# Pairs of channel tiles by Strassen's products, and down sums in DRAM, in layer 0's FFN of a two-layer backbone

## The chip, the cores and the metric

The kernel runs on one core of one Trainium2 chip. The metric is the device time of one execution in microseconds. The engines are named as in the profile: PE (TensorE), DVE (VectorE), ACT (ScalarE), POOL (GpSimd) and SP (SyncE, which only issues DMAs here).

## What is computed

Two layers of a trunk over 256 latent and 256 context tokens, 2048 wide, float32. Layer 0 has a pooling mixer, layer 1 neighbourhood attention; each is followed by a gated FFN (5504 wide) with a depthwise convolution over three neighbouring tokens on its gate. In layer 0 both streams go through the FFN:

```python
def conv_ffn(u, w_gate, w_up, conv_w, conv_b, w_down):
    T = u.shape[1]
    gp = jnp.pad(u @ w_gate, ((0, 0), (1, 1), (0, 0)))
    gte = gp[:, :T] * conv_w[0] + gp[:, 1:T + 1] * conv_w[1] + gp[:, 2:] * conv_w[2] + conv_b
    return (jax.nn.silu(gte) * (u @ w_up)) @ w_down
...
    for i in range(DEPTH):
        ml = (silu_c @ w_mod[i] + b_mod[i]).reshape(B, 6, 1, D)
        mc = (silu_cc @ w_mod[i] + b_mod[i]).reshape(6, 1, 1, D)
...
        h = h + ml[:, 5] * conv_ffn(modulate(rms_norm(h, norm2_g[i]), ml[:, 3], ml[:, 4]),
                                    ffn_w_gate[i], ffn_w_up[i], ffn_conv_w[i], ffn_conv_b[i], ffn_w_down[i])
        if not last:
...
            hc = hc + mc[5] * conv_ffn(modulate(rms_norm(hc, norm2_g[i]), mc[3], mc[4]),
                                       ffn_w_gate[i], ffn_w_up[i], ffn_conv_w[i], ffn_conv_b[i], ffn_w_down[i])
```

## The kernel before

All products are done in a short float format, fp32r, with each operand split into a high part and the rest (hi and lo). A product is three matmuls: hi with hi, hi with lo, lo with hi. A weight tile comes by a DMA of 512 KB (128x1024, `load`, L127), ACT casts it to the high part (L143), and DVE subtracts that from it for the low part (L145). The tokens lie as 16 tiles A0 to A15 of 128 features by 512 columns (256 latent, 256 context), hi and lo, made by `normalise` (L304 to L317).

The FFN of layer 0 has 43 channel tiles f of 128. `gu0(f)` does gate and up of one tile, each 16 input tiles × 3 matmuls of 128x512 (L631 to L633) into one PSUM bank. `gate0` (L362 to L380) makes the convolution and the product on ACT and DVE: a scaled copy (L364), two additions of the shifted bank (L366, L368), Silu (L371), times up (L372), split in hi and lo (L378, L379). Gate and up of tiles 0 to 7 are done earlier, in another form; the change touches tiles from 11 on.

`down0(c, ...)` takes a chunk of four channel tiles: for each of 16 output tiles, 4 × 3 matmuls of 128x512 (L657 to L659). ACT scales each half of the result (latent, context) by the modulation (L669), and POOL adds it to the residual streams hl and hc, which lie in SBUF (L670). The last chunk adds on DVE instead (L663) and starts the next norm. The main loop (L674 to L702) does gate and up of chunk c, then down of chunk c − 1.

Beside this runs a pump, `mod_pairs`: modulation rows of layer 1, made on DVE. One step loads 512 KB of `wmod` and multiplies and adds it into `macc`, by four operations of 512 columns or one of 1024 (L239, L241); at a row's end come transposes (L251) and reduces (L252). The generator is advanced at written places in `gu0` and `down0`.

Buffers around the change: six places for loaded weights, of which the pump has three in this stage; four pairs of hi and lo tiles (128x1024); seven tiles for the FFN's activations; PSUM with four banks for gate and up and four for down. Each engine works through its own queue in order. A scheduler sets that order when the program is built; a tile that is reused makes its next writer wait.

Of the kernel before, what the change touches and what calls it, by code (L numbers as in the profile page):

```python
# [10 lines left out]
F32 = mybir.dt.float32  # L11
F32R = mybir.dt.float32r
AF = mybir.ActivationFunctionType
ALU = mybir.AluOpType
# [3 lines left out]
P = 128  # L18
D = 2048
KT = D // P  # L20
T = 256
F = 5504
NF = F // P
H = 32
W = 64
# [5 lines left out]
NS = 8  # L31
# [26 lines left out]
def kernel(ctx: ExitStack, tc: tile.TileContext, xT, cxT, wmod, wg, wu, wd, wp,  # L58
                         wq, wv, wo, vec, cc, rope, inv, strips, out):
    nc = tc.nc  # L60
    main = ctx.enter_context(tc.tile_pool(name="main", bufs=1))
    wst = ctx.enter_context(tc.tile_pool(name="wst", bufs=1))
    whp = ctx.enter_context(tc.tile_pool(name="whp", bufs=3))
# [34 lines left out]
    hl = main.tile([P, KT, T], F32, name="hl")  # L98


    extra = []
    turn = [0]

    hold = []

# [15 lines left out]
    def load(src, cols, name):  # L121

        ts = []
        for j in range(0, cols, 1024):
            n = min(1024, cols - j)
            t = stage(f"{name}_{j}")
            nc.sync.dma_start(t[:, :n], src(j, j + n))  # L127
            ts.append((t, n))
        return ts

    def split(ts, name, share=0):

        parts = []
        for j, (t, n) in enumerate(ts):
            turn[0] += 1
            pools = [whp] * 3 + extra
            pool = pools[turn[0] % len(pools)]
            hi = pool.tile([P, 1024], F32R, tag="wh", name=f"{name}h{j}")
            lo = pool.tile([P, 1024], F32R, tag="wl", name=f"{name}l{j}")
            with ExitStack() as behind:  # L140
                for ins in hold:
                    behind.enter_context(tc.issue_after(ins))
                nc.scalar.copy(hi[:, :n], t[:, :n])  # L143
                eng = nc.gpsimd if share and turn[0] % share == 0 else nc.vector
                eng.tensor_tensor(lo[:, :n], t[:, :n], hi[:, :n].bitcast(F32), op=ALU.subtract)  # L145
            parts.append((hi, lo))
        return parts
# [7 lines left out]
    both = (0, 1)  # L155
# [146 lines left out]
    A = {}  # L302
# [15 lines left out]

    chunks = [list(range(f, min(f + 4, NF))) for f in range(0, NF, 4)]


    v_first = []
    with ExitStack() as ph0:
        p0 = ph0.enter_context(tc.tile_pool(name="p0", bufs=1, reuse_waits="tile"))
        f0 = ph0.enter_context(tc.tile_pool(name="f0", bufs=6, reuse_waits="tile"))
        hc = p0.tile([P, KT, T], F32, name="hc")
# [7 lines left out]
        def h_of(s):  # L334
            return hc if s else hl
# [2 lines left out]
            return f0.tile([P, 2, 512], dt, tag="act", bufs=7, name=name)  # L338

        PART = {}  # L340
        sc = p0.tile([P, KT, 32], F32, name="sc")
# [278 lines left out]
        def gu0(f):  # L620
            res = []
            for nm, wsrc in (("g", wg), ("u", wu)):
                parts = ld(wsrc[0, f], f"w{nm}0_{f}")
                if f > NS + 3:
                    next(pump, None)
                ps = bank("gu", f"{nm}0_{f}")
                for k in range(KT):
                    hi, lo = parts[k // 8]
                    c = P * (k % 8)
                    xh, xl = flat(A[k][:, 0]), flat(A[k][:, 1])  # L630
                    nc.tensor.matmul(ps, hi[:, c : c + P], xh, start=(k == 0), stop=False)  # L631
# [8 lines left out]

        def down0(c, fs, acts, after=None):
            n = len(fs)
            last = c == len(chunks) - 1
            for mg in range(4):
                parts = split(load(lambda a, b: wd[0, mg, :, fs[0] + a // 512 : fs[0] + b // 512, :], 512 * n, f"wd0_{c}_{mg}"),
                              f"wd0_{c}_{mg}")
                if c > 1:
                    next(pump, None)
                for m in range(4):
                    if m == 2 and c > 1:  # L650
                        next(pump, None)
                    ps = bank("d", f"d0_{c}_{mg}_{m}")
                    for i in range(n):
                        hi, lo = parts[i // 2]
                        o = 512 * (i % 2) + P * m
                        xh, xl = acts[i]
                        nc.tensor.matmul(ps, hi[:, o : o + P], xh, start=(i == 0), stop=False)  # L657
                        nc.tensor.matmul(ps, hi[:, o : o + P], xl, start=False, stop=False)  # L658
                        nc.tensor.matmul(ps, lo[:, o : o + P], xh, start=False, stop=(i == n - 1))  # L659
                    k = 4 * mg + m  # L660
                    if last:
                        for s in both:
                            nc.vector.scalar_tensor_tensor(h_of(s)[:, k, :], ps[:, T * s : T * s + T], M(0, 5, k, s),  # L663
                                                           h_of(s)[:, k, :], op0=ALU.mult, op1=ALU.add)
                        n3.add(h_of, k)
                    else:
                        y = f0.tile([P, 2, T], F32, tag="t2", name=f"dy{c}_{k}")
                        for s in both:
                            nc.scalar.activation(y[:, s], ps[:, T * s : T * s + T], AF.Copy, scale=M(0, 5, k, s))  # L669
                            nc.gpsimd.tensor_tensor(h_of(s)[:, k, :], h_of(s)[:, k, :], y[:, s], op=ALU.add)  # L670
                if after is not None:
                    after()

# [2 lines left out]
        acts[NC], sg = gate0(NC, *r6)  # L676
        normalise(0, 3, h_of, both, rstd, f0, range(14, KT))
        res = gu0(NS)
        rest = [e for e in range(NS) if e not in acts]

        def more():
# [3 lines left out]

        while rest and rest[0] < 4:
            more()
        down0(0, chunks[0], [acts[f] for f in chunks[0]], more)
        while rest:
            more()  # L690
        acts[NS], sg = gate0(NS, *res)
        for c, fs in enumerate(chunks):
            if c < 2:
                continue
            fs = [f for f in fs if f > NS]
            for f in fs:
                acts[f], sg = gate0(f, *gu0(f))
            down0(c - 1, chunks[c - 1], [acts[f] for f in chunks[c - 1]])
        prev = (len(chunks) - 1, chunks[-1], [acts[f] for f in chunks[-1]])
        down0(*prev)  # L700
        for _ in pump:
            pass  # L702
# [529 lines left out]
```

## Time and profile before

| | |
|---|---|
| median of 3 runs | 3102.39 us (3102.04 to 3103.3) |
| the profiled execution | 3103.48 us, of which its span is 3101.7 us |
| mean granted TensorE clock | 0.993 |
| busy time of PE, DVE, ACT, POOL | 3030.0, 1932.6, 1373.2, 826.1 us |
| gate, up and down of layer 0 in the main loop | about 500 to 1710 us of the span |

A row of a group gives the line, engine, operation, the tiles written and read with buffer numbers left out, and the count; then either busy time and mean, or the least, median and longest duration in ns. A row of a timeline has start and length in us, and in brackets how long the engine was idle before and what ended that. Durations overlap a little at their ends, so the pitch from start to start is what an engine really spends.

### The profile page before, as it was taken

What the parts mean: (1) busy time and instruction counts of PE and PEld (TensorE: products, weight loads), DVE (VectorE), ACT (ScalarE), POOL (GpSimd) and SP (SyncE); (2) the same over time, 40 slices, a digit from 0 to 9 for tenths busy, and PEclk for the clock granted to TensorE, in tenths of its full rate; (3) what the DMA queues carried; (4) which work ended last, traced back from release to release, by engine and by line L of the source; (5) the groups of instructions that cost most, each with busy time, mean ns of one, the idle gap of its engine ahead of it and who ended that gap; (6) DMA issues with size and microseconds to landing.
All of it is one profiled execution on the core that took longest, in us unless ns stands there. A gap on an engine that the chain in (4) does not pass through costs nothing.

```text
span 3101.7 us, 40819 instructions
## 1 busy us (share of the span) xinstructions
PE 3030.0 (98%) x15082; PEld 2414.3 (78%) x15082; DVE 1932.6 (62%) x2748; ACT 1373.2 (44%) x2219; POOL 826.1 (27%) x823
## 2 busy tenths in 40 slices
PE   6999899999999999999999999999999999999998
PEld 2565558888888888888888788878788888888887
DVE  4445674285765848567485665564777666666666
ACT  3333454333233332323334444343545666656665
POOL 2011213213031230302213000000002466556665
PEclk9999999999999999999999999999999999999999
DMA  9978573264846657475573333332345565555563
GB/s 376 333 271 306 177 246 102 89 217 149 251 141 206 198 162 247 133 225 171 182 226 118 102 113 106 102 114 96 111 153 179 177 196 188 192 189 185 179 195 117
DMA packets 177927, 559.70 MB, mean 180 GB/s; under 512 B 17600, under 2 KB 22208, under 8 KB 177728
## 3 DMA queue, kind: packets, MB, share of 16 engines
q1 hardware_dynamic: 177728, 557.10, 55.0%
q8 instruction: 119, 1.95, 0.3%
q14 instruction: 80, 0.66, 0.1%
HBM read 554.93 MB, written 2.10 MB: 180 GB/s over the span
## 4 chain that ended last, share of the span: by engine, by line
PE 94%; DMA 2%; DVE 2%; POOL 1%; ACT 1%; issue 0%; SPq 0%; DVEq 0%; ACTq 0%; POOLq 0%
PE g L766 5%; PE u L766 5%; PE d L657 5%; PE d L659 5%; PE d L658 5%; PE d L813 4%; PE u L631 4%; PE u L632 4%; PE u L633 4%; PE g L631 4%; PE g L633 4%; PE g L632 4%; PE mod L193 3%; PE u L769 3%; PE g L769 3%; PE d L817 2%
## 5 line engine op out<-in xcount | busy, mean ns | idle before, releaser
L670 POOL TENSOR_TENSOR hl<-hl,dy 128x256 f32<-128x256 f32 x160 | 149.0, 931 | 958.6 <-ACT dy L669 957.3
L828 POOL TENSOR_TENSOR hl<-hl,dy 128x256 f32<-128x256 f32 x320 | 331.5, 1069 | 188.4 <-ACT dy L826 186.1
L241 DVE SCALAR_TENSOR_TENSOR macc<-wm,sc,macc 128x512 f32<-128x512 f32 (+1 forms) x360 | 325.2, 935 | 68.6 <-DMA wm<-wmod 67.6
L669 ACT ACTIVATE dy<-d,modT 128x256 f32<-128x256 f32 x320 | 133.5, 470 | 196.8 <-PE d L659 195.5
L193 PE MATMUL mod<-wm,sc 128*32 128x512 f32 x768 | 134.6, 618 | 26.6 <-DMA wm<-wmod 26.5
L670 POOL TENSOR_TENSOR hc<-hc,dy 128x256 f32<-128x256 f32 x160 | 126.0, 787 | 0.0
L145 DVE TENSOR_TENSOR wd_2l<-wd,wd_2h 128x1024 fp32r<-128x1024 f32 (+1 forms) x44 | 53.9, 1229 | 112.8 <-ACT wd_2h L143 112.8
L826 ACT ACTIVATE dy<-d,modT 128x512 f32<-128x512 f32 x160 | 104.4, 683 | 42.7 <-PE d L817 41.2
L915 POOL TENSOR_TENSOR rk<-rk,rp 128x256 f32<-128x256 f32 x16 | 13.2, 826 | 365.4 <-DVE rk L914 309.8
L145 DVE TENSOR_TENSOR wd_3l<-wd,wd_3h 128x1024 fp32r<-128x1024 f32 (+1 forms) x44 | 52.0, 1202 | 80.6 <-ACT wd_3h L143 80.6
L145 DVE TENSOR_TENSOR wd_1l<-wd,wd_1h 128x1024 fp32r<-128x1024 f32 (+1 forms) x44 | 53.7, 1224 | 58.6 <-ACT wd_1h L143 58.6
L466 POOL TENSOR_TENSOR pf<-ws,inv 128x256 f32<-128x256 f32 x32 | 27.7, 886 | 222.4 <-DVE ws L461 154.7
L193 PEld LDWEIGHTS mod<-wm,sc 128*32 128x32 f32 x768 | 23.6, 110 | 81.0 <-issue 59.4
L143 ACT CAST wd_1h<-wd 128x1024 fp32r<-128x1024 f32 (+1 forms) x44 | 45.2, 1029 | 79.8 <-PE u L632 50.6
L145 DVE TENSOR_TENSOR wd_0l<-wd,wd_0h 128x1024 fp32r<-128x1024 f32 (+1 forms) x44 | 54.6, 1247 | 40.7 <-ACT wd_0h L143 40.6
L1004 ACT ACTIVATE sb<-sb,nm 128x512 f32<-128x512 f32 x64 | 46.1, 721 | 64.4 <-DVE nm L1000 63.2
L143 ACT CAST wd_0h<-wd 128x1024 fp32r<-128x1024 f32 (+1 forms) x44 | 45.3, 1031 | 57.9 <-PE u L766 29.1
L792 DVE TENSOR_TENSOR actb<-sgb,actb 128x256 fp32r<-128x256 f32 x43 | 52.3, 1216 | 27.0 <-ACT actb L791 27.0
L657 PE MATMUL d<-act,wd_2h 128*128 128x512 f32 x172 | 68.0, 395 | 0.0
L658 PE MATMUL d<-act,wd_2h 128*128 128x512 f32 x172 | 67.9, 395 | 0.0
L657 PE MATMUL d<-act,wd_3h 128*128 128x512 f32 x172 | 67.9, 395 | 0.0
L657 PE MATMUL d<-act,wd_0h 128*128 128x512 f32 x172 | 67.9, 395 | 0.0
(1752 smaller groups left out, 9286.1 us busy)
## 6 DMA issues: line engine op xcount, KB each, us to landing
wm<-wmod SPq DMA_DIRECT2D x384, 512.0 KB, 6.1
wd<-wd SPq DMA_DIRECT2D x168, 512.0 KB, 4.4
wg<-wg SPq DMA_DIRECT2D x156, 512.0 KB, 4.6
wu<-wu SPq DMA_DIRECT2D x156, 512.0 KB, 4.5
wv<-wv SPq DMA_DIRECT2D x32, 512.0 KB, 3.9
wk<-wq SPq DMA_DIRECT2D x32, 512.0 KB, 4.0
wq<-wq SPq DMA_DIRECT2D x32, 512.0 KB, 3.7
wo<-wo SPq DMA_DIRECT2D x32, 512.0 KB, 4.4
```

The lines of the kernel that those rows point to most:

```text
L145: eng.tensor_tensor(lo[:, :n], t[:, :n], hi[:, :n].bitcast(F32), op=ALU.subtract)
L193: nc.tensor.matmul(ps[32 * j : 32 * j + 32, :], sc[:, 4 * g + j, :], ts[j // 2][0][:, 512 * (j % 2) : 512 * (j % 2) + 512], start=(g == 0) ...
L241: nc.vector.scalar_tensor_tensor(acc[s], v, sc2[:, k, s : s + 1], acc[s], op0=ALU.mult, op1=ALU.add)
L631: nc.tensor.matmul(ps, hi[:, c : c + P], xh, start=(k == 0), stop=False)
L632: nc.tensor.matmul(ps, hi[:, c : c + P], xl, start=False, stop=False)
L633: nc.tensor.matmul(ps, lo[:, c : c + P], xh, start=False, stop=(k == KT - 1))
L657: nc.tensor.matmul(ps, hi[:, o : o + P], xh, start=(i == 0), stop=False)
L658: nc.tensor.matmul(ps, hi[:, o : o + P], xl, start=False, stop=False)
L670: nc.gpsimd.tensor_tensor(h_of(s)[:, k, :], h_of(s)[:, k, :], y[:, s], op=ALU.add)
L766: nc.tensor.matmul(ps, hi[:, c : c + P], flat(B[k]), start=(k == 0), stop=False)
L769: nc.tensor.matmul(ps[:, T:], lo[:, c : c + P], B[k][:, 0], start=False, stop=(k == KT - 1))
L828: nc.gpsimd.tensor_tensor(hl[:, k, :], hl[:, k, :], y[:, q], op=ALU.add)
```

## The change

**Pairs.** From tile 11 on, gate and up are done for two channel tiles at once (`pair0`). The inputs' first eight tiles are four pairs of feature blocks (i, i + 4), times the two streams, so the 128x512 products of these tiles form a 2 × 2 block product: two weight blocks by two channel tiles, two feature blocks by two streams. It is done by Strassen's seven products of 128x256 columns (Winograd's form with shared sums). The other eight input tiles are multiplied as before (`others`), with 128x512.

For it, the sums of the weight blocks are made on POOL, in place in the loaded tiles: four subtractions of 128x512 per gate or up (L779, L780, L782, L785). Each of eleven blocks is split in hi and lo by itself (`half`, L765 on ACT, L766 on DVE, 128x512). The products 1, 7, 6 and 5 go to two banks of the down group, which ACT copies to SBUF (L825); POOL adds these up (L829 to L832, 128x256), and DVE adds them to the two banks (L844). The corresponding sums of the inputs are made once, after tile 10 (`sums`).

**Residual.** SBUF for those sums comes from the residual: hl and hc are copied to DRAM (`hd`) at the start of the main loop, and down's results are added to them there by DMAs from POOL's queue that accumulate (L694, 256 KB each, 160 in all). ACT writes the results into five buffers in turn. `back` reads hl and hc again in the last but one down. Chunks are called runs, and are now 0–3, 4–7, 8–10, then four each.

The diff, cut to its core:

```diff
-                            nc.gpsimd.tensor_tensor(h_of(s)[:, k, :], h_of(s)[:, k, :], y[:, s], op=ALU.add)
+                        nc.gpsimd.dma_start(out=hd[:, :, k, :], in_=y, accum_op=ALU.add)
+                if c == len(runs) - 2 and mg:
+                    back(mg - 1)
...
+        def away_with(*what):
+            with tc.issue_after(latest[0]):
+                for s, g in what:
+                    nc.sync.dma_start(hd[:, s, 4 * g : 4 * g + 4, :], h_of(s)[:, 4 * g : 4 * g + 4, :])
+        away_with((1, 2), (1, 3))
...
+        ys = p0.tile([P, KT // 2, T], F32, tag="hc1", name="dys")
+        away = [ys[:, 2 * i : 2 * i + 2, :] for i in range(4)]
+        away.append(p0.tile([P, 2, T], F32, tag="sc", name="dyz"))
...
+        def half(v, name):
...
+            t = pool.tile([P, 1024], F32R, tag=tag, name=name)
+            hi, lo = t[:, :JC], t[:, JC:]
+            nc.scalar.copy(hi, v)
+            nc.vector.tensor_tensor(lo, v, hi.bitcast(F32), op=ALU.subtract)
+            return hi, lo
+        def pair0(f):
+            res = []
+            for nm, wsrc in (("g", wg), ("u", wu)):
+                x, y, c1, c2 = [load(lambda a, b: wsrc[0, f + e][:, j + a : j + b], 1024, f"w{nm}0_{f + e}_{j}")[0][0]
+                                for j in (0, 1024) for e in (0, 1)]
+                b11, b21, b12, b22 = x[:, :JC], x[:, JC:], y[:, :JC], y[:, JC:]
+                W = {}
+                W[1] = half(b11, name + "b11")
+                nc.gpsimd.tensor_tensor(b11, b12, b11, op=ALU.subtract)
+                nc.gpsimd.tensor_tensor(b12, b22, b12, op=ALU.subtract)
+                W[7] = half(b12, name + "t3")
+                nc.gpsimd.tensor_tensor(b12, b22, b11, op=ALU.subtract)
+                W[6] = half(b12, name + "t2")
+                W[5] = half(b11, name + "t1")
+                nc.gpsimd.tensor_tensor(b11, b21, b12, op=ALU.subtract)
...
+                for j, (m, n) in enumerate(((1, 7), (6, 5))):
+                    ps = bank("d", f"e{j}{nm}_{f}")
+                    product(m, ps[:, :T], True, True)
+                    product(n, ps[:, T:], True, True)
+                    e = f0.tile([P, 2, T], F32, tag="t2", name=f"e{j}{nm}_{f}")
+                    nc.scalar.copy(flat(e), ps)
...
+                nc.gpsimd.tensor_tensor(e2[:, 0], e2[:, 0], e1[:, 0], op=ALU.add)
+                nc.gpsimd.tensor_tensor(e1[:, 1], e1[:, 1], e2[:, 0], op=ALU.add)
+                nc.gpsimd.tensor_tensor(e2[:, 0], e2[:, 0], e2[:, 1], op=ALU.add)
+                nc.gpsimd.tensor_tensor(e2[:, 1], e2[:, 1], e1[:, 1], op=ALU.add)
+                next(pump, None)
+                others(0, 0, True, False)
+                product(2, b1[:, :T], False, False)
+                product(4, b1[:, T:], False, False)
...
+                for ps, e in ((b1, e1), (b2, e2)):
+                    nc.vector.tensor_tensor(ps, ps, flat(e), op=ALU.add)
```

The program is built from this, and the order on each engine is what the scheduler makes of it. Three places follow.

On DVE, beside gate and up of tile 22 before. The rows are the pump's macc, weight subtracts (wg, wu) and the steps of the gate:

```order
L239 TENSOR_SCALAR macc_1_12_7183<-wm1_12_0_7091,sc2_81 128x1024
L145 TENSOR_TENSOR wg0_22l1_7178<-wg0_22_1024_7171,wg0_22h1_7177 128x1024
L241 SCALAR_TENSOR_TENSOR macc_1_12_7183<-wm1_12_1_7122,sc2_81,macc_1_12_7183 128x1024
L366 SCALAR_TENSOR_TENSOR g1_21_7159<-g0_21_7024,vt_70,g1_21_7159 128x2x255
L241 SCALAR_TENSOR_TENSOR macc_1_12_7183<-wm1_12_2_7181,sc2_81,macc_1_12_7183 128x1024
L368 SCALAR_TENSOR_TENSOR g1_21_7159<-g0_21_7024,vt_70,g1_21_7159 128x2x255
L241 SCALAR_TENSOR_TENSOR macc_1_12_7183<-wm1_12_3_7217,sc2_81,macc_1_12_7183 128x1024
L145 TENSOR_TENSOR wu0_22l0_7249<-wu0_22_0_7244,wu0_22h0_7248 128x1024
```

On DVE after, where the second pair of the same run (tiles 21 and 22) goes from gate to up. The hu21 rows are halves of up's blocks, g0_21 and g0_22 the banks of the gate:

```order
L766 TENSOR_TENSOR hu21_c00_7866<-wu0_21_1024_0_7846,hu21_c00_7866 128x512
L766 TENSOR_TENSOR hu21_t3_7855<-wu0_22_0_0_7844,hu21_t3_7855 128x512
L766 TENSOR_TENSOR hu21_b21_7869<-wu0_21_0_0_7842,hu21_b21_7869 128x512
L242 SCALAR_TENSOR_TENSOR macc_1_12_7678<-wm1_12_12_8159,sc2_81,macc_1_12_7678 128x1024
L844 TENSOR_TENSOR g0_21_7687<-g0_21_7687,e0g_21_7714 128x512
L844 TENSOR_TENSOR g0_22_7688<-g0_22_7688,e1g_21_7741 128x512
L242 SCALAR_TENSOR_TENSOR macc_1_12_7678<-wm1_12_13_8194,sc2_81,macc_1_12_7678 128x1024
L766 TENSOR_TENSOR hu21_t2_7859<-wu0_22_0_0_7844,hu21_t2_7859 128x512
L766 TENSOR_TENSOR hu21_t4_7872<-wu0_21_0_0_7842,hu21_t4_7872 128x512
```

The weight subtracts are half as wide and stand closer. The t2 half, which PE takes as the third product of up, stands behind the two additions into the gate's banks, and so behind PE's end of that gate.

On POOL before, while the down product of the fifth chunk runs (dy is ACT's result, hl and hc are the residual):

```order
L670 TENSOR_TENSOR hl_84<-hl_84,dy4_0_7493 128x256
L670 TENSOR_TENSOR hc_91<-hc_91,dy4_0_7493 128x256
L670 TENSOR_TENSOR hl_84<-hl_84,dy4_1_7511 128x256
L670 TENSOR_TENSOR hc_91<-hc_91,dy4_1_7511 128x256
L670 TENSOR_TENSOR hl_84<-hl_84,dy4_2_7532 128x256
```

On POOL after, while gate and up of tiles 21 and 22 run, and at the begin of the down product behind them:

```order
L782 TENSOR_TENSOR wg0_22_0_0_7633<-wg0_22_0_0_7633,wg0_21_0_0_7631 128x512
L785 TENSOR_TENSOR wg0_21_0_0_7631<-wg0_21_0_0_7631,wg0_22_0_0_7633 128x512
L829 TENSOR_TENSOR e1g_21_7741<-e1g_21_7741,e0g_21_7714 128x256
L830 TENSOR_TENSOR e0g_21_7714<-e0g_21_7714,e1g_21_7741 128x256
L831 TENSOR_TENSOR e1g_21_7741<-e1g_21_7741 128x256
L832 TENSOR_TENSOR e1g_21_7741<-e1g_21_7741,e0g_21_7714 128x256
L779 TENSOR_TENSOR wu0_21_0_0_7842<-wu0_22_0_0_7844,wu0_21_0_0_7842 128x512
L780 TENSOR_TENSOR wu0_22_0_0_7844<-wu0_22_0_0_7844 128x512
L782 TENSOR_TENSOR wu0_22_0_0_7844<-wu0_22_0_0_7844,wu0_21_0_0_7842 128x512
```

POOL's work has gone from beside the down products to beside gate and up, and has become subtractions of weights and sums of products; in down it issues DMAs.

On SP before, at the start of the main loop (wu and wd are weights of up and down):

```order
L127 DMA wu0_8_0_3662<-wu 128x1024
L127 DMA wd0_0_0_0_3723<-wd 128x1024
L127 DMA wd0_0_1_0_3823<-wd 128x1024
L127 DMA wd0_0_0_1024_3725<-wd 128x1024
L127 DMA wd0_0_1_1024_3825<-wd 128x1024
```

And after, with hd the residual in DRAM:

```order
L128 DMA wu0_8_0_3666<-wu 128x1024
L710 DMA hd_93<-hc1_95 128x1024 x2
L128 DMA wd0_0_0_0_3731<-wd 128x1024
L128 DMA wd0_0_1_0_3825<-wd 128x1024
L128 DMA wd0_0_0_1024_3733<-wd 128x1024
L710 DMA hd_93<-hc0_94 128x1024
L710 DMA hd_93<-hl_84 128x1024
L128 DMA wd0_0_1_1024_3827<-wd 128x1024
```

Copies to DRAM stand ahead of and between the loads of the first down product.

More of the change, by code (lines that the diff above doesn't have):

```diff
@@ L319 @@
     chunks = [list(range(f, min(f + 4, NF))) for f in range(0, NF, 4)]
+    runs = [[*range(4)], [*range(4, 8)], [8, 9, 10]] + [list(range(f, f + 4)) for f in range(11, NF, 4)]
     v_first = []
@@ L340 @@
         PART = {}
-        sc = p0.tile([P, KT, 32], F32, name="sc")
+        sc = p0.tile([P, KT, 32], F32, tag="sc", name="sc")
         nc.gpsimd.memset(sc, 0.0)
@@ L678, with back @@
         res = gu0(NS)
+        def away_with(*what):
[3 more added lines that the diff above has]
+        away_with((1, 2), (1, 3))
+        def back(g):
+            for s in both:
+                nc.gpsimd.dma_start(out=h_of(s)[:, 4 * g : 4 * g + 4, :], in_=hd[:, s, 4 * g : 4 * g + 4, :])
+        ys = p0.tile([P, KT // 2, T], F32, tag="hc1", name="dys")
@@ L687 @@
             more()
-        down0(0, chunks[0], [acts[f] for f in chunks[0]], more)
+        down0(0, runs[0], [acts[f] for f in runs[0]], more)
         while rest:
```

126 lines of the change are left out of this document (113 added, 13 removed).

## Prediction

> **What bounds the kernel now.** I read the page's list of engines and its chain that ended last, then the windows over the layer 0 FFN, then the rows of each engine there.
>
> ```profile
> PE 3030.0 (98%) x15082; PEld 2414.3 (78%) x15082; DVE 1932.6 (62%) x2748; ACT 1373.2 (44%) x2219; POOL 826.1 (27%) x823
> PE 94%; DMA 2%; DVE 2%; POOL 1%; ACT 1%; issue 0%; SPq 0%; DVEq 0%; ACTq 0%; POOLq 0%
> ```
>
> TensorE is busy for 98% of the span and makes up 94% of the chain. For the stretch in which the change acts stand two windows (columns: window, length, then PE, PEld, DVE, ACT, POOL, granted clock, DMA share, GB/s):
>
> ```profile
> 588.00:1630.00 1042.00, 1042.00 (x4558) 853.19 (x4557) 682.63 (x850) 358.12 (x538) 213.27 (x256) 1.00 0.61 190
> 655.00:700.00 45.00, 45.00 (x200) 37.02 (x199) 38.26 (x46) 11.71 (x14) 0.00 (x0) 1.00 0.83 255
> ```
>
> PE has no hole in 1042 us. A matmul saved there is time saved, as long as nothing else becomes late. Second comes DVE: 66% over the stretch, 85% (38.26 of 45.00) in a part where gate and up run beside the pump of modulation rows.
>
> **What PE saves.** The pitches come from the gate/up line and from the timeline of layer 1's down product:
>
> ```profile
> L631 PE MATMUL u<-A,wu_9h x16: 389/390/404, 532.1 to 542.5; 128*128 128x512 f32 x16
> L631 PE MATMUL g<-A,wg_10h x16: 389/389/389, 543.1 to 553.3; 128*128 128x512 f32 x16
> ```
> ```profile
> 3073.08 0.28 PE L811 MATMUL d<-actb,wd_0l 128*128 128x256 f32 x1
> 3073.20 0.28 PE L809 MATMUL d<-actb,wd_0h 128*128 128x256 f32 x1
> ```
>
> From the first L631 of u to that of the next g lie 48 matmuls and 543.1 − 532.1 = 11.0 us: 0.2292 each. The narrow ones start 0.120 apart. A gate (or up) of two channel tiles is 96 × 0.2292 = 22.00 us before. After, it is 7 products × 12 matmuls = 84 × 0.120 = 10.08, and the upper eight input tiles as they were, 48 × 0.2292 = 11.00: 21.08. It saves 0.92 us, where an eighth of half the work would be 1.38, since 0.120 is more than half of 0.2292. 16 pairs × 2 make **29.5 us**. PE has no other work less or more.
>
> **What DVE and POOL get in return.** Pitches of DVE, from its timeline beside gate and up, start to start:
>
> ```profile
> 657.65 0.68 DVE L379 TENSOR_TENSOR act<-sg,act 128x512 fp32r<-128x512 f32 x1
> 658.25 2.07 DVE L241 SCALAR_TENSOR_TENSOR macc<-wm,sc,macc 128x512 f32<-128x512 f32 x3
> ...
> 663.36 1.29 DVE L251 STREAM_TRANSPOSE modu<-macc 128x512 f32<-128x512 f32 x2
> 664.58 0.64 DVE L252 TENSOR_REDUCE modr<-modu 128x16 f32<-128x512 f32 x1
> ...
> 667.18 0.74 DVE L239 TENSOR_SCALAR macc<-wm,sc 128x1024 f32<-128x1024 f32 x1
> 667.84 0.74 DVE L366 SCALAR_TENSOR_TENSOR g<-g,vt,g 128x510 f32<-128x510 f32 x1
> 668.50 1.27 DVE L241 SCALAR_TENSOR_TENSOR macc<-wm,sc,macc 128x1024 f32<-128x1024 f32 x1
> 669.69 0.74 DVE L368 SCALAR_TENSOR_TENSOR g<-g,vt,g 128x510 f32<-128x510 f32 x1
> ...
> 677.19 0.68 DVE L372 TENSOR_TENSOR sg<-sg,u 128x512 f32<-128x512 f32 x1
> 677.79 0.68 DVE L181 TENSOR_TENSOR modT<-modt_0s,vt 32x8 f32<-32x8 f32 x4
> 678.50 1.23 DVE L145 TENSOR_TENSOR wu_14l<-wu,wu_14h 128x1024 fp32r<-128x1024 f32 x1
> 679.64 1.28 DVE L241 SCALAR_TENSOR_TENSOR macc<-wm,sc,macc 128x1024 f32<-128x1024 f32 x1
> ```
>
> So a 512-wide subtract costs 0.60, a product with PSUM 0.60, a 1024-wide macc 1.19, a 1024-wide subtract 1.14, a gate step 0.66, a transpose 0.61, a reduce 0.64, four modT rows 0.71. A run of four channel tiles had 16 subtracts of 1024 (18.2 us); it gets 44 of 512 (26.4) and 8 additions into PSUM (4.8): DVE goes from about 86 us per run (66% of PE's 132.0) to 99, PE from 132.0 to 128.3 (4 × 21.08 + 44.0 of down). On average that fits. POOL drops its 32 additions of 256 per run and gets 16 subtracts of 512, 16 additions of 256 and 16 DMA issues. Their rows:
>
> ```profile
> L352 POOL TENSOR_TENSOR part<-part,n2acc x12: 1272/1452/2187, 364.6 to 447.6; 128x512 f32<-128x512 f32 x12
> L670 POOL TENSOR_TENSOR hl<-hl,dy x160: 729/738/1682, 480.7 to 1674.4; 128x256 f32<-128x256 f32 x160
> ```
>
> With 1.40 and 0.74 that is 34 us per run, after 24. All but the issues now lies in the 84 us of gate and up, and between DVE rows: t3 needs POOL's second subtract, t2 its third, t4 its fourth.
>
> What happens when DVE and POOL meet stands in two places of the timeline of before:
>
> ```profile
> 599.24 1.23 DVE L145 TENSOR_TENSOR wd_2l<-wd,wd_2h 128x1024 fp32r<-128x1024 f32 x1 [0.18 <-ACT wd_2h L143]
> 599.72 1.34 POOL L670 TENSOR_TENSOR hl<-hl,dy 128x256 f32<-128x256 f32 x1 [2.07 <-ACT dy L669]
> ```
> ```profile
> 633.00 0.80 POOL L670 TENSOR_TENSOR hl<-hl,dy 128x256 f32<-128x256 f32 x1 [1.99 <-ACT dy L669]
> 633.12 1.76 DVE L145 TENSOR_TENSOR wu_12l<-wu,wu_12h 128x1024 fp32r<-128x1024 f32 x1
> 633.76 1.72 POOL L670 TENSOR_TENSOR hc<-hc,dy 128x256 f32<-128x256 f32 x1
> ```
>
> The addition that starts inside a subtract takes 1.34 instead of 0.73, ending 0.59 after the subtract; the subtract that starts inside an addition takes 1.76 instead of 1.23. Operations of this kind do not run at once: they queue. In "SBUF — State Buffer", section "Who interferes with whom", the Trainium skill says that a DVE instruction with two SBUF inputs contends with a GpSimd instruction that reads SBUF, and with one SBUF input it does not; the rows agree for the first half. By that rule the stretch below ends at least 2.5 us late and the sum is 3095 or more; without it POOL's work would cost DVE nothing and the sum would be 3075.
>
> **The tight place.** I count DVE's order from the addition into g_20 (second tile of the first pair of a run, L844) to the t2 half of the next pair's up, L766. T = 0 is where PE ends that gate. PE then needs t2 after one up, one gate and two products: 21.08 + 21.08 + 24 × 0.120 = 45.0. DVE's 53 rows are 21 subtracts (12.6), 13 macc (15.5), 5 additions (3.0), 4 gate steps (2.6), 4 of products and act (2.4), 5 of the macc's end and start (3.2), modT (0.7): **40.0 us**. POOL has between them 8 additions and 7 subtracts: 5.9 + 9.8 = 15.7. A wait is near the start: the c10 tile's load takes the room that the t4 half frees. Landing of loads:
>
> ```profile
> wm<-wmod SPq DMA_DIRECT2D x384, 512.0 KB, 6.1
> wd<-wd SPq DMA_DIRECT2D x168, 512.0 KB, 4.4
> wg<-wg SPq DMA_DIRECT2D x156, 512.0 KB, 4.6
> ```
>
> About 4.5 to land and 0.6 for ACT's cast, less two DVE rows: at most 3.9, nothing if t4 ran early; I take 2.4. Without POOL the stretch ends at 40.0 + 2.4 = 42.4, 2.6 ahead of need. If only the 29.3 us of two-input rows (subtracts, macc, two act rows) exclude POOL, and the rest overlaps it perfectly, it is 29.3 + 15.7 + 2.4 = 47.4, 2.4 late. With no overlap it is 58.1, 13.1 late. POOL's rows come when their inputs do, not when DVE has a harmless one, so the middle: I take **8 us per run**. The next down product clears the lag: beside its 44.0 us DVE has 8 subtracts of 1024 (9.1), a third of the run's 24 pump steps (8 × 4 × 0.66 + 16 × 1.19 = 40.2, so 13.4) and a few rows of the gates. Eight runs have pairs: **64 us**, bounds 0 and 8 × 14.6 = 117 (3.9 in place of 2.4).
>
> **The residual in DRAM.** Each of 160 output tiles was two POOL additions (1.5 us) and becomes one accumulating DMA of 256 KB from POOL's queue. No run here shows an accumulate. The nearest row is a plain one:
>
> ```profile
> wd<-wd SPq DMA_DIRECT2D x8, 256.0 KB, 2.7
> ```
>
> An output tile comes every 12 × 0.2292 = 2.75 us and there are five buffers, so a transfer may take some 11 us before ACT waits for a buffer; behind ACT's waiting copy stand the casts of the next weights, and then PE. Read and write double the row's bytes: 2.7 to 6, hidden; I take nothing. The issue on POOL binds only above (44.0 − 5.6) / 16 = 2.4 us each, 5.6 being the next pair's four subtracts, which queue between them. The Trainium skill ("DMA: Bandwidth & Descriptors", section "Anatomy of one DMA — SWDGE (gpsimd) path") gives such a DMA 2.0 us and one more per 436e3 bytes, an estimated 2.6 here for a plain one; the sum is the same by either.
>
> At the start two copies of 512 KB to DRAM stand on SP's queue ahead of wd_0:
>
> ```profile
> 450.38 28.89 SPq L127 DMA_DIRECT2D wd<-wd  x7
> ```
> ```profile
> 461.05 1.04 ACT L143 CAST wd_0h<-wd 128x1024 fp32r<-128x1024 f32 x1
> ```
>
> The load could land at 454.8 and is cast at 461.05; behind the cast ACT has the last two input tiles of gate 8. Two copies of 4.4 make it 2.6 late if one follows the other, nothing if they overlap: 1 us. Six more copies fall in down0's first pass, whose loads have such slack too. The sums for Strassen's inputs (8 rows of 512 and 16 of 256 on POOL, 8 × 1.40 + 16 × 0.74 = 23 us) lie beside the down product of the second run, 44 us, in which POOL has else only issues: nothing; without that cover, 23. Reading the residual back lies before the last down product's 44 us: nothing.
>
> **Sum.** The profiled execution took 3103.48 (span 3101.7 and 1.8 outside), 1.1 above the median of 3102.39. 3103.5 − 29.5 + 64 + 1 = **3139**.
>
> **Rivals.** (1) POOL is covered: its rows fall beside DVE's one-input rows and idle time, and the loads come early; stalls of 0 to 2.8 per run. For it: DVE idles on PE and DMA in all rows quoted, and 42.4 is under 45.0. Against it: 599.72 and 633.12. All hidden it is 3103.5 − 29.5 + 1 = 3075. It decides at 28.5 / 8 = 3.6 us per run, where the gain is gone. (2) About half hidden, 2.8 to 4.3 per run: 3097 to 3109, no change. (3) Heavier: after such a stall PE runs slow. In the n3 norm, where PE waits for DVE, the windows show
>
> ```profile
> 1718.00:1721.00 3.00, 3.00 (x8) 2.01 (x7) 3.00 (x9) 3.00 (x9) 0.00 (x0) 0.50 0.00 0
> ```
>
> Eight matmuls in 3.00 us at a clock of 0.50, against 13 at 0.2292: about 1.2 us lost per 3 us of it. Stalls of 12 to 14.6 with that, 8 × 13.2 to 8 × 15.8 on 3075: 3181 to 3201. The Trainium skill ("TensorE: Matmul & The Clock Gate", section "What's actually happening") puts the drop after an idle window of about 3.4 us; no wait of PE in the rows quoted tests that length, and my 8 us are split over two or three waits, some near it.
>
> **How the numbers follow.** The stall of 4.3 to 12 is the likeliest, 0.52 (own range 3109 to 3171); (1) 0.26; (2) 0.11; (3) or a POOL queue that binds, 0.11. A measurement of this kernel can tell about 0.2%, 6 us, from no change. Faster 0.26, same 0.11, slower 0.63. The range, 3075 to 3178, leaves out most of (3) and a little below.
>
> **What would show it.** Right: PE holes of 2 to 5 us ahead of L805 to L807, released by DVE's subtract for t2 or t3, mostly in the second pair of a run; longer means than 0.68 for L766 and than 1.27 for L779 to L785; PE's busy time down by about 30. Wrong: PE without holes there (rival 1), holes released by ACT or a DMA, waits of POOL between accumulating DMAs, or a clock below 0.9 in the windows of the pairs.

## The result, and the profile after

The changed kernel takes 3171.27 us (median of 4 runs, 3167.07 to 3175.35); the one before took 3102.38 beside it. The ratio is 1.0221, with an interval from 1.0204 to 1.0239: 2.2% slower. Its profiled execution (3167.07 us) has a span of 3165.3 us, 63.6 more than before, and a mean granted clock of 0.985 after 0.993. The page's list of engines and its chain now read:

```profile
PE 3034.8 (96%) x16234; PEld 2465.1 (78%) x16234; DVE 2139.4 (68%) x3048; ACT 1476.3 (47%) x2519; POOL 1084.8 (34%) x951
...
PE 70%; DVE 11%; DMA 10%; issue 4%; POOL 3%; ACT 2%; SPq 0%; DVEq 0%; POOLq 0%; ACTq 0%
```

PE was 94% of the chain and is 70%. Its idle time is the span less its busy time: 71.7 us before, 130.5 now, 58.8 more. Its busy time is 4.8 us higher, though 29.5 us of pitch are gone, so 34.3 us more of busy time lie on the same work: 58.8 + 34.3 − 29.5 = 63.6. The windows show both (columns as before), first over the pairs, then around five holes:

```profile
600.00:1760.00 1160.00, 1096.91 (x5930) 945.99 (x5930) 909.73 (x1196) 477.87 (x867) 468.59 (x396) 0.98 0.80 211
```
```profile
660.00:665.00 5.00, 0.89 (x4) 0.46 (x3) 4.93 (x10) 1.66 (x3) 0.23 (x1) 0.78 0.42 93
665.00:670.00 5.00, 5.00 (x25) 4.92 (x25) 4.97 (x8) 1.66 (x4) 0.00 (x0) 0.54 0.52 97
...
695.00:700.00 5.00, 2.83 (x16) 2.18 (x15) 2.58 (x3) 2.58 (x5) 0.36 (x1) 1.00 0.96 328
700.00:705.00 5.00, 5.00 (x30) 4.33 (x29) 4.93 (x5) 1.78 (x3) 4.75 (x4) 1.00 0.90 308
...
810.00:815.00 5.00, 0.00 (x0) 0.00 (x0) 2.18 (x3) 0.34 (x1) 0.00 (x0) 0.80 1.00 328
815.00:820.00 5.00, 4.67 (x11) 3.70 (x12) 4.69 (x6) 2.32 (x5) 2.96 (x3) 0.52 0.74 250
...
831.00:834.00 3.00, 0.92 (x4) 0.30 (x2) 3.00 (x4) 2.29 (x5) 0.67 (x1) 0.91 0.10 37
834.00:837.00 3.00, 3.00 (x14) 3.00 (x15) 3.00 (x5) 0.00 (x0) 0.00 (x0) 0.52 0.86 157
...
1496.00:1499.00 3.00, 0.36 (x4) 0.16 (x2) 3.00 (x4) 2.02 (x5) 1.11 (x1) 1.00 0.78 164
1499.00:1502.00 3.00, 3.00 (x15) 3.00 (x16) 3.00 (x5) 0.39 (x2) 0.00 (x0) 0.51 0.52 115
```

Where there was no hole in 1042 us, there are 63 us in 1160. Behind 4.1 us of idle PE the clock is 0.54 for the next five microseconds, behind more than 5 us 0.52. Shorter holes go both ways: behind 2.2 us at 696 it stays at 1.00, behind 2.1 us at 832 and 2.6 us at 1496 it is 0.52 and 0.51 over the next 3 us.

The clock doesn't explain all of the 34.3 us. By the mean granted clocks it is some 26 us (0.015 × 3165.3 less 0.007 × 3101.7, an estimate), and less where PE stood idle meanwhile. The edges of the holes add to busy time even at a clock of 1.00:

```profile
695.63 0.28 PE L807 MATMUL u<-A,hu_t 128*128 128x256 f32 x1
698.09 0.50 PE L815 MATMUL u<-A,hu_c 128*128 128x512 f32 x1 [2.17 <-ACT hu_c L765]
698.43 0.39 PE L816 MATMUL u<-A,hu_c 128*128 128x512 f32 x1
```

The last matmul ahead of the hole counts 0.28 us where its pitch is 0.12, and the first one behind it takes 0.34 to the next where 0.23 is usual: 0.27 us per hole. For the 36 waits of the next list that makes about 10 us, an estimate too.

The waits of PE between 600 and 1760 us name who releases the holes (total, times, longest, in us):

```profile
PE e1g L807 <- DVE hg_t L766: 15.2, 9, 4.1
PE e1u L807 <- DVE hu_t L766: 12.4, 5, 3.3
PE g L815 <- ACT hg_c L765: 9.3, 6, 5.5
PE e1u L805 <- ACT hu_t L765: 7.8, 8, 1.8
PE e0u L807 <- DVE hu_t L766: 7.4, 6, 1.8
PE u L815 <- ACT hu_c L765: 3.6, 2, 2.2
```

It is the t halves (t2 and t3) on DVE or ACT, 42.8 us in these rows, and a c block (by PE's order c10), whose cast waits for its load, 12.9. Another 5.1 us, in one place near 745 us, are released by ACT's copies into the dy buffers. Groups of DVE and POOL there show stretched operations:

```profile
L242 DVE SCALAR_TENSOR_TENSOR macc<-wm,sc,macc 128x1024 f32<-128x1024 f32 x120 | 180.8, 1507 | 19.1 <-DMA wm<-wmod 18.2
...
L766 DVE TENSOR_TENSOR hg_t<-wg,hg_t 128x512 fp32r<-128x512 f32 x64 | 62.6, 986 | 40.0 <-ACT hg_t L765 39.6
```
```profile
L785 POOL TENSOR_TENSOR wg<-wg,wg 128x512 f32<-128x512 f32 x16 | 29.1, 1819 | 1.2 <-DVE hg_t L766 0.7
```

The macc of 1024 had a mean of 1282 ns and has 1507; a t half takes 986 where the same form alone takes 680; POOL's fourth subtraction takes 1819, where the shortest POOL row of that size before (L352) took 1272. One hole in the timeline, of DVE and then of POOL, shows how these meet:

```profile
1377.94 1.28 DVE L242 SCALAR_TENSOR_TENSOR macc<-wm,sc,macc 128x1024 f32<-128x1024 f32 x1 [3.30 <-DMA wm<-wmod]
1379.14 1.29 DVE L766 TENSOR_TENSOR hu_t<-wu,hu_t 128x512 fp32r<-128x512 f32 x2
1380.35 2.30 DVE L242 SCALAR_TENSOR_TENSOR macc<-wm,sc,macc 128x1024 f32<-128x1024 f32 x1
1382.58 1.76 DVE L766 TENSOR_TENSOR hu_b<-wu,hu_b 128x512 fp32r<-128x512 f32 x1
```
```profile
1379.91 1.66 POOL L782 TENSOR_TENSOR wu<-wu,wu 128x512 f32<-128x512 f32 x1 [2.45 <-DVE hu_t L766]
1381.65 2.14 POOL L785 TENSOR_TENSOR wu<-wu,wu 128x512 f32<-128x512 f32 x1
```

DVE stands 3.30 us for a load of the pump; the halves of t3 and t1 behind it come late by that; POOL's third subtraction waits 2.45 for them; then DVE's macc and POOL's subtractions stretch each other. The t2 half, which PE waits for, comes only at 1386.06.

### The profile page after: what moved, and what is told of

It is laid out like the page before. It is cut to its first block, busy times and chain, and to the rows that moved or that the text cites. A ratio compares the mean times of both kernels' runs of the same rounds, so it can differ in the third digit from the quotient of the medians.

```text
span 3165.3 us, 44092 instructions
## 1 busy us (share of the span) xinstructions
PE 3034.8 (96%) x16234; PEld 2465.1 (78%) x16234; DVE 2139.4 (68%) x3048; ACT 1476.3 (47%) x2519; POOL 1084.8 (34%) x951
## 4 chain that ended last, share of the span: by engine, by line
PE 70%; DVE 11%; DMA 10%; issue 4%; POOL 3%; ACT 2%; SPq 0%; DVEq 0%; POOLq 0%; ACTq 0%
PE g L944 5%; PE u L944 5%; PE d L991 4%; PE d L677 4%; PE d L678 4%; PE d L679 4%; DVE macc L242 3%; DMA wm<-wmod 3%; PE mod L194 3%; DMA wu<-wu 3%; PE g L947 3%; PE u L947 3%; DMA wg<-wg 2%; PE d L995 2%; PE k L1119 2%
## 5 line engine op out<-in xcount | busy, mean ns | idle before, releaser
L1006 POOL TENSOR_TENSOR hl<-hl,dy 128x256 f32<-128x256 f32 x320 | 331.5, 1070 | 188.4 <-ACT dy L1004 186.1
L242 DVE SCALAR_TENSOR_TENSOR macc<-wm,sc,macc 128x512 f32<-128x512 f32 (+1 forms) x360 | 356.1, 1028 | 35.2 <-DMA wm<-wmod 34.3
L694 POOL DMA_DIRECT2D hd<-dys x116 | 132.2, 1171 | 235.8 <-ACT dys L693 231.6
L693 ACT ACTIVATE dys<-d,modT 128x256 f32<-128x256 f32 x232 | 97.1, 471 | 120.9 <-PE d L679 64.9
L815 PE MATMUL g<-A,hg_c 128*128 128x512 f32 x256 | 102.6, 401 | 9.4 <-ACT hg_c L765 9.3
L815 PE MATMUL u<-A,hu_c 128*128 128x512 f32 x256 | 102.9, 402 | 3.8 <-ACT hu_c L765 3.6
L765 ACT CAST hu_t<-wu 128x512 fp32r<-128x512 f32 x64 | 38.9, 620 | 138.7 <-POOL wu L780 52.3
L816 PE MATMUL u<-A,hu_c 128*128 128x512 f32 x256 | 102.0, 398 | 0.0
L817 PE MATMUL u<-A,hu_c 128*128 128x512 f32 x256 | 101.8, 397 | 0.0
L816 PE MATMUL g<-A,hg_c 128*128 128x512 f32 x256 | 101.5, 397 | 0.0
L817 PE MATMUL g<-A,hg_c 128*128 128x512 f32 x256 | 101.3, 396 | 0.0
L766 DVE TENSOR_TENSOR hg_t<-wg,hg_t 128x512 fp32r<-128x512 f32 x64 | 62.6, 986 | 40.0 <-ACT hg_t L765 39.6
L766 DVE TENSOR_TENSOR hu_t<-wu,hu_t 128x512 fp32r<-128x512 f32 x64 | 55.1, 876 | 32.9 <-ACT hu_t L765 31.8
```

The lines of the kernel that those rows point to most:

```text
L242: nc.vector.scalar_tensor_tensor(acc[s], v, sc2[:, k, s : s + 1], acc[s], op0=ALU.mult, op1=ALU.add)
L694: nc.gpsimd.dma_start(out=hd[:, :, k, :], in_=y, accum_op=ALU.add)
L815: nc.tensor.matmul((b1, b2)[e], hi[:, c : c + P], xh, start=(first and i == 0), stop=False)
L816: nc.tensor.matmul((b1, b2)[e], hi[:, c : c + P], xl, start=False, stop=False)
L817: nc.tensor.matmul((b1, b2)[e], lo[:, c : c + P], xh, start=False, stop=(last and i == J - 1))
L1006: nc.gpsimd.tensor_tensor(hl[:, k, :], hl[:, k, :], y[:, q], op=ALU.add)
```

## The experiments

Theory A is the prediction's: POOL's sums and DVE's operations with two SBUF inputs queue for each other (the expectations call this the lock), and DVE's order is late for the t halves. Rival B: DVE's in-order queue is late by itself, with macc rows that wait for their loads ahead of the halves. Rival C: the accumulating DMAs crowd the loads. Rival D, which came up with the memset kernels below: POOL's steps are simply long, and the chain from load to t2 and t4 with them. The scheduler orders each engine's rows anew in every kernel, so an edit can change the order too.

**Fewer pump steps beside the pairs.**

```diff
-                if c > 1:
-                    next(pump, None)
-                    if m == 2 and c > 1:
+                    if c > 1:
                         next(pump, None)
...
                 C[1, 1] = half(c2[:, JC:], name + "c11")
-                next(pump, None)
...
                 product(4, b1[:, T:], False, False)
-                next(pump, None)
```

> Two of the four pump steps of each gate or up of a pair are moved to the down products, which get 16 steps in place of 8; all the work is done. The changed kernel has 63 us of holes on PE between 600 and 1760 us and loses about 27 us more to a lower clock behind them; without both it would be at 3103.5 - 29.5 = 3074. Theory A (POOL's sums and DVE's two-input rows queue for each other, so that DVE is late for the t halves): with 8 of 24 steps less, 13 us of DVE less beside a run's two pairs, the holes fall to 25 or less and the clock loss to 10: 3095 to 3112. Theory B (no lock matters; DVE's in-order queue is late because macc rows that wait for their loads stand ahead of the halves): the same fall or more, 3080 to 3100. Theory C (accumulating DMAs crowd the loads): more loads fall into the down products, where the DMA share is already above 1, so it stays at 3150 or more.

Measured: 3217.29 us, ratio 1.0376 (1.0359 to 1.0393), slower than the changed kernel by 46 us. The forecasts of A and B fell; C's, 3150 or more, held, though the runs without accumulating DMAs below speak against C. DVE's waits between 560 and 1800 us show where the time went:

```profile
DVE macc L242 <- DMA wm<-wmod: 126.2, 61, 5.9
```

DVE waits 126 us for the pump's loads and does so in order; PE now waits 36 us ahead of the first products of a gate (e0g), where it waited 1.7. That these loads compete in the down products with weights and accumulating DMAs is a likely reason, not shown here. Here DVE's row count fell beside the pairs and the holes grew, so the sum of pitches alone doesn't say where DVE is late.

**POOL writes without reading.** Twice: the eight sums as one memset each, and as two or two and a half, to make up their length.

```diff
-                nc.gpsimd.tensor_tensor(b11, b12, b11, op=ALU.subtract)
+                nc.gpsimd.memset(b11, 0.0)
...
-                nc.gpsimd.tensor_tensor(e2[:, 0], e2[:, 0], e1[:, 0], op=ALU.add)
+                nc.gpsimd.memset(e2[:, 0], 0.0)
```

> POOL's four weight subtractions and four sums of products per gate or up become memsets of the same tiles, so that POOL writes and no longer reads SBUF; the products are then not Strassen's, and the output isn't the reference's. The waits for POOL stay. Theory A (lock): holes of 63 us fall to 20 or less, means of the halves' subtracts fall from 0.72 to 0.99 us to about 0.68, time 3080 to 3105. Theory B (macc rows waiting for loads ahead of the halves): holes stay at 40 or more, 3130 to 3165. Theory C (accumulating DMAs): unchanged, 3155 to 3170.

> As in the memset kernel (3076), but each subtraction of 128x512 is two and a half memsets, each sum of 128x256 two, so that POOL is busy for about as long as with the sums (1.06 to 1.36 and 0.62 us, after 1.29 and 0.74), still without reading SBUF; the output isn't the reference's. Theory A (the lock): near the memset kernel, 3076 to 3100. Rival D (it was the length of POOL's steps in the chain from load to t2 and t4, not the lock, and the memset of 0.53 us made it short): back to 3145 to 3170.

Measured: 3076.33 and 3097.52 us (one run each). The page's engines, of the short memsets and then of the long:

```profile
PE 3001.3 (98%) x16234; PEld 2447.9 (80%) x16234; DVE 2041.6 (66%) x3048; ACT 1476.5 (48%) x2519; POOL 864.6 (28%) x951
```
```profile
PE 3012.6 (97%) x16234; PEld 2453.9 (79%) x16234; DVE 2039.4 (66%) x3048; ACT 1472.5 (48%) x2519; POOL 1005.0 (32%) x1335
```

With the short ones PE's busy time is 28.7 under the kernel before, the 29.5 of the pitches, and its idle time 73.0 against 71.7: the prediction's 3075 for a stall that is all hidden. With POOL's length made up, 21 us come back; against the changed kernel's profiled run (3167.07) 70 us stay away. So most of the loss goes when POOL's operations no longer read SBUF, and rival D's 3145 to 3170 fell; A's forecasts held, the first but for 4 us. Theory B's fell too: DVE's macc rows still wait 25 us for loads in the first of the two. Two things are not parted by this. A memset doesn't need the second operand, so the first step no longer waits for the second tile's load; in the changed kernel POOL stood 14.4 us in all for loads ahead of that step (L779, 600 to 1750 us). And the order on DVE is another one: matched by the names of the tiles they write, some 6% of its 3048 rows stand elsewhere than in the changed kernel. Against the order alone speaks the kernel with c01 first, below, with 7%, its own edit included, and 3156.81 us.

**No accumulating DMAs, and the DRAM part alone.**

```diff
-                        nc.gpsimd.dma_start(out=hd[:, :, k, :], in_=y, accum_op=ALU.add)
```

> The 160 accumulating DMAs of down's results are left out, so that the FFN's sum of all runs but the last is missing from the output. Theory A: only the holes released by ACT's copies into the dy buffers go (about 5 us near 745 us), and POOL's subtractions start without standing behind issues of 1.09 us: 3150 to 3165. Theory B: loads land earlier in the down products, not beside the pairs: 3150 to 3165. Theory C: the loads of weights and modulation land at 4.4 and 6.1 us again and most holes go: 3085 to 3115.

Measured: 3161.64 us (one run), as A and B said: the 5.1 us released by the dy copies are gone, and the t halves and c blocks still hold PE up. The second kernel does all gates and ups the old way:

```diff
-                for f in fs[::2]:
-                    for e, banks in enumerate(pair0(f)):
-                        acts[f + e], sg = gate0(f + e, *banks)
+                if f > NS:
+                    acts[f], sg = gate0(f, *gu0(f))
```

> All gates and ups as before the change, no Strassen and no sums; the residual in DRAM with its copies, accumulating DMAs and reading back stays. Theories A and B: no holes, since DVE has its old work and POOL only issues: 3101 to 3108, the time before within 0.2%. Theory C: holes from late loads remain, 3120 or more.

Measured: 3097.97 us, ratio 0.999 (0.9981 to 1.0), 3 us under the kernel before, at the edge of what can be told. Its window over the old stretch:

```profile
588.00:1630.00 1042.00, 1042.00 (x4559) 853.25 (x4559) 678.08 (x857) 354.06 (x535) 134.92 (x124) 1.00 0.81 223
```

No hole, with a DMA share of 0.81 in place of 0.61. Rival C is out: without the pairs the residual in DRAM costs nothing, and with them leaving out its DMAs won some 5 us (3161.64 after 3167.07 in the profiled run).

**The sums on DVE.** All eight, or the four subtractions only, with `nc.vector` for `nc.gpsimd` in `pair0`.

```diff
-                nc.gpsimd.tensor_tensor(b11, b12, b11, op=ALU.subtract)
+                nc.vector.tensor_tensor(b11, b12, b11, op=ALU.subtract)
```

> The four subtractions and four sums of each gate or up go from POOL to DVE; all is computed. DVE gets 16 x 0.60 + 16 x 0.40 = 16 us more per run, POOL loses 34. Theory A: since the two exclude each other, 34 us of POOL for 16 of DVE shortens what must queue; the stretch of 40.0 + 2.4 us becomes 49.8, 4.8 late at the most: holes of 15 to 38 us, clock loss about 10: 3095 to 3125. If the lock played no part, DVE's 16 us more make it later than with POOL: 3170 or more. Rival D: the steps become shorter (0.60 for 1.29), 3090 to 3130, so this run parts A and D from B only.

> Only the four weight subtractions go to DVE, the sums of products stay on POOL; all is computed. Theory A: DVE's stretch is 40.0 + 7 x 0.60 + 2.4 = 46.6, 1.6 late, and POOL's 8 sums in it cost up to 5.9 more: 2 to 7.5 per run, clock loss up to 10: 3090 to 3140. If the lock played no part and DVE's queue alone did: 3165 or more.

Measured: 3183.84 us, ratio 1.0262 (1.0242 to 1.0282), and 3183.4, ratio 1.0266 (1.0249 to 1.0283): slower than with POOL, and a plain miss of A's forecast and of D's. They lie where the forecasts put them if the lock played no part. With all eight on DVE its operations are no longer stretched, and yet its busy time is about what it was; groups and PE's waits between 600 and 1750 us:

```profile
L766 DVE TENSOR_TENSOR hg_t<-wg,hg_t 128x512 fp32r<-128x512 f32 x62 | 42.0, 684 | 3.4 <-ACT hg_t L765 3.3
```
```profile
PE g L815 <- ACT hg_c L765: 24.8, 6, 6.6
PE u L815 <- ACT hu_c L765: 13.2, 5, 3.9
```

DVE is busy for 913 us of this window, 902 with the sums on POOL: what the lock took from it, its new work takes. The forecast set 34 us of POOL per run against 16 of DVE; but POOL's time had cost DVE only about what its rows stretched by, (986 − 684) ns × 64 for hg_t, (1507 − 1282) ns × 120 for the macc and so on over the groups of L766 and L242, some 92 us in all or 12 per run. The holes move to c10, whose load waits for the t4 half.

**Room for c10, and c10 later.**

```diff
-        ring = range(NW // 2 + 1, NW + 1)
+        ring = range(NW // 2 + 2, NW + 1)
```

> The pump's ring has two places in place of three, the weights' four in place of three, so that the load of c10 needn't wait for the t4 half; all is computed. If late loads of the weights set the holes: the 13 us of PE that ACT's casts of c blocks released go and the t halves come earlier, 3120 to 3150. Theory A: the holes released by the t halves stay, and the pump, with one load ahead, stalls DVE for longer: 3150 to 3190.

Measured: 3185.43 us (one run): the waits for the c blocks' casts are nearly gone, but a fourth place for weights, taken from the pump, is paid for by DVE, which waits 121 us for the pump's loads in place of 34. The other way is to use c01 first:

```diff
                 product(4, b1[:, T:], False, False)
                 next(pump, None)
+                others(0, 1, False, True)
                 others(1, 0, True, False)
                 product(3, b2[:, :T], False, False)
-                others(0, 1, False, True)
                 others(1, 1, False, True)
```

> In each gate or up the block c01, which comes from a tile loaded early, is split and multiplied ahead of c10, whose load waits for the t4 half; all is computed. If the late load of c10 is a part of its own beside the lock: the 13 us of PE that ACT's casts of c blocks released go, with some clock, 3140 to 3160. If it only shows the lag that the t halves make, it moves to the t halves: 3160 to 3175.

Measured: 3156.81 us, ratio 1.0182 (1.0166 to 1.0197), 14 less than the changed kernel. The late load is a part of its own, and a small one.

**The accumulator in PSUM**, by itself and with c01 first.

```diff
-                acc = mp.tile([P, 1024], F32, tag="macc", bufs=1, name=f"macc_{l}_{ch}")
-                acc = [acc, acc] if m == 2 else [acc[:, 0:512], acc[:, 512:1024]]
+                split_d[0] = True
+                acc = [pp.tile([P, 512], F32, tag=f"d{i}", bufs=1, name=f"macc{i}_{l}_{ch}") for i in range(2)]
```

> The pump's accumulator moves from SBUF to two PSUM banks, so that its macc rows have one SBUF input in place of two; the down products, e products and modulation sums have two banks in place of four; ACT copies the accumulator out for the transposes; all is computed. Theory A (lock): of the 29.3 us of two-input rows in DVE's tight stretch 15.5 no longer exclude POOL, so 13.8 + 15.7 stay, the lag falls to 0 to 4 us per run: 3080 to 3125, with the remaining cost from two banks fewer (ACT's copies must come within 2.75 us). If the lock plays no part: DVE's work is the same or more and PE has fewer banks, 3165 or more.

> The two edits together, accumulator in PSUM and c01 ahead of c10; all is computed. Theory A: 3078 to 3115, below the kernel before if two banks fewer cost less than 10 us. If the lock plays no part: 3150 or more.

Measured: 3168.42 us, ratio 1.022 (1.0204 to 1.0235), and 3155.38, ratio 1.0192 (1.0168 to 1.0216). Nothing won by moving the accumulator, and both lie where the forecasts put them if the lock played no part. The macc and the t halves of the first of the two:

```profile
L255 DVE SCALAR_TENSOR_TENSOR macc<-wm,sc,macc 128x512 f32<-128x512 f32 x479 | 338.4, 747 | 59.4 <-DMA wm<-wmod 58.9
L781 DVE TENSOR_TENSOR hg_t<-wg,hg_t 128x512 fp32r<-128x512 f32 x62 | 61.1, 996 | 30.6 <-ACT hg_t L780 29.9
```

The macc is no longer stretched (747 is what it took per 512 columns without POOL). PE's waits for t halves fell from 42.8 us to about 21. But DVE waits 59 us for the pump's loads in place of 34, the t halves' subtracts are stretched as before, PE's waits for c blocks' casts rose from 12.9 to 22.6, and it waits some 15 us for rows that empty its fewer banks. Other waits took the place of those that went.

**One pair per run.** Only the pair behind the down product by Strassen, and c01 first.

```diff
-                for f in fs[::2]:
-                    for e, banks in enumerate(pair0(f)):
-                        acts[f + e], sg = gate0(f + e, *banks)
+                for e, banks in enumerate(pair0(fs[0])):
+                    acts[fs[e]], sg = gate0(fs[e], *banks)
+                for f in fs[2:]:
+                    acts[f], sg = gate0(f, *gu0(f))
```

> Only the first pair of each run, the one behind the down product, is done by Strassen; the other two tiles go by the old gate and up. Since these need the inputs unchanged, the fourth input sum gets the space of the dy buffers, and dy uses the shared temporaries and one buffer more; c01 stands ahead of c10 as in the run before; all is computed. PE saves half of 29.5, 14.7 us. Theory A (DVE's rows plus POOL's rows that exclude them, against PE's time): per run DVE loses 8 additions' and sums' worth of the lock, and the down product's slack lies right ahead of the pair; holes fall from 63 us to 15 or less and the clock loss to 5: 3086 to 3102, the first of these kernels at or under the one before. If the holes come with each pair by itself (its chain from load to t2, whatever DVE has queued): half of 63 and of 27 stay, 3125 to 3135.

Measured: 3169.59 us, ratio 1.0216 (1.0201 to 1.023). Both forecasts fell. Windows through one run, whose pair lies from 1168 to 1217 us:

```profile
1180.00:1200.00 20.00, 18.06 (x95) 15.39 (x93) 19.45 (x25) 5.66 (x10) 6.69 (x4) 0.91 0.43 134
1200.00:1220.00 20.00, 15.21 (x89) 12.57 (x87) 14.74 (x23) 5.44 (x7) 5.85 (x4) 1.00 0.80 235
1220.00:1240.00 20.00, 18.12 (x73) 14.93 (x74) 18.93 (x26) 7.05 (x10) 0.00 (x0) 0.91 0.90 236
...
1260.00:1280.00 20.00, 20.00 (x88) 16.15 (x87) 8.38 (x9) 7.58 (x13) 3.27 (x3) 1.00 0.78 204
1280.00:1300.00 20.00, 20.00 (x88) 16.27 (x87) 3.31 (x3) 8.83 (x18) 8.22 (x8) 1.00 0.95 190
```

DVE is full inside the pair up to 1200 us (19.45 of 20.00) and nearly idle in the down product (3.31). In the pair's last part, with a hole of PE of 2.39 us, it is not full (14.74): it stands 3.62 us for the cast of a c block, whose load is late. The 18.93 belong to the old gate behind the pair. PE has 51 us of holes where there were 63; 12.9 of them are new, the old gate's wait for a gate row of the pair on DVE (L386) that comes late. So holes arise inside the 42 us of a single pair, behind a down product in which DVE has slack, and a run's average doesn't show them.

## Why the prediction was right, and where it was short

The forecast of 3139 was 36 us above the kernel before; the measured change is 69. The result lies inside the range (3075 to 3178), at the very end of the likeliest branch's own (3109 to 3171): the sum had no term for 34 us of the change, and the width of the range took them in. Of the signs that the prediction named, the holes ahead of L805 to L807 and the longer means came; PE's busy time, which should have fallen by about 30, rose by 4.8. Two signs against it came as well: ACT released about 26 us of the holes (the 7.8 of t halves, the 12.9 of c blocks, the 5.1 of dy copies), and the clock fell to 0.5 behind holes of the pairs.

**PE's saving** of 29.5 us was right: 28.7 in the run with short memsets.

**The stall of 8 us per run, 64 in all,** was right in size: PE's idle time rose by 58.8. Its place was the one named, the t halves, with c10 second. From 900 us on the holes lie in the last 50 us or so ahead of each down product, the second pair, as named; before that they lie in both pairs. The size is partly luck: 8 was the middle between 2.4 and 13.1 (2.4 by its sum; another of its sentences says 2.5), and it rests on a bound that later forecasts didn't bear out.

**The lock** was right as the row that stretches, by the means of L766 and L785. Replacing POOL's reads by writes of like unstretched length took 70 us away. As a sum it was wrong in use: the bound "29.3 + 15.7" treated POOL's and DVE's times as exchangeable, and forecasts built on it missed in six kernels (fewer pump steps, sums on DVE twice, accumulator in PSUM twice, one pair). In four of them (sums on DVE twice, accumulator in PSUM twice) the time lay where it was expected if the lock played no part. So the lock is one limit among several. What these kernels point to in its place is a pair as a whole at its limit: DVE full over much of it, its macc rows waiting for loads in order, three places for weights, and four dependent steps from load to t4. Where one was eased, another set the end. How the 70 us divide between the lock, the wait for the second operand and the order that the scheduler chose stays open; an order written by hand for DVE was not tried.

**The slower PE around the holes** is the term that was too small. The sum had nothing for it; it stood in the third rival, at 1.2 us per run and only for stalls of 12 us and more. It is 34.3 us, 4.3 per run, at stalls of the forecast size: some 26 at most by the clock, about 10 at the holes' edges. 3139 with it would have been 3173. The rows at 660 and 810 us show that behind one hole of 4 us or more the clock is near half for some 5 us, those at 832 and 1496 that a hole of 2 to 3 us can be enough. The Trainium skill ("TensorE: Matmul & The Clock Gate", section "What's actually happening") gives an idle window of about 3.4 us. The holes of 2.2 and 4.1 us lie on either side of that, but those of 2.1 and 2.6 us don't agree with it, and the measurement decides: in this trace the length of a hole alone doesn't tell whether the clock falls.

**The start** was put at 1 us and cost none: PE is busy for 159.12 of the 160 us from 440 to 600 in both traces.

**The accumulating DMA** was nearly hidden, though its bound of 6 us was wrong. Its rows, from the page and from the view of `hd`:

```profile
hd<-dys POOLq DMA_DIRECT2D x116, 256.0 KB, 8.1
```
```profile
L694 POOL DMA_DIRECT2D hd<-dys x116: 1078/1087/3429, 484.0 to 1591.9; - x116
```

It lands after 8.1 us in the median and its issue takes POOL 1.09, under the 2.4 at which it would bind. The longest landing, 15.2 us, is above the 11 us that the five buffers allow: near 745 us ACT waits for buffers, and PE stands 5.1 us behind it. The sum had nothing for this.

## What to carry to other kernels

A saving on the engine that bounds the kernel is kept only if the engines that feed it have slack inside the stretch where the work lies, not on average over a stage. Before moving work to POOL, look whether DVE's operations there read two inputs from SBUF, and count both sides' stretch. When a forecast has holes of 2 us and more on PE, put the slower matmuls behind them into the sum.

## What the runs showed of the hardware

An accumulating DMA of 256 KB to DRAM took 3.9 to 15.2 us to land (median 7.9 over all of them), against 2.7 for a plain load of that size before the change; 160 of them cost no time in the kernel without pairs, and 5.1 us of holes in the one with them. POOL's memset of 128x512 takes 0.53 us alone, a subtraction of two SBUF tiles 1.29. Moving DVE's accumulator to PSUM ended the stretch of its macc (747 ns per 512 columns), while subtractions with two SBUF inputs kept theirs (996 ns, where 684 is usual without POOL's reads).
